# A hybrid decoder step on one core: early splits for the last matrix product, and squares of the final norm by halves

## The chip, the cores and the metric

The kernel runs on one core of a Trainium2 chip. The metric is the device time of one execution in microseconds (us). A core has TensorE (PE, matrix products), VectorE (DVE), ScalarE (ACT), GpSimd (POOL) and SyncE (SP, which issues most DMAs); each works through its own queue in order, and they wait for one another by semaphores.

## The reference

One inference step of a one-layer decoder for 1024 new prompt tokens (behind 16 meta tokens) and 32 tokens of eight running sequences. Attention and a state-space mixer are added into the residual stream `h`; then come the squared-ReLU MLP and a last RMSNorm, which is where the change lies:

```python
def mix_and_mlp(h, ao, so, attn_out_g, w_out, norm2_g, w_up, w_down):
    mix = jnp.concatenate([rmsnorm(ao, attn_out_g), so], axis=-1)
    h = h + mix @ w_out
    u = jax.nn.relu(rmsnorm(h, norm2_g) @ w_up)
    return h + (u * u) @ w_down          # w_down: 4096 x 1024
...
y_prompt = rmsnorm(hp, norm_f_g)[:, N_META:]   # x / sqrt(mean(x*x) + 1e-6) * g, over 1024 features
y_sample = rmsnorm(hs, norm_f_g)
```

Everything is float32.

## The kernel before

Activations lie features by tokens: 128 features on the partitions, eight feature blocks `m` = 0 to 7, 1056 tokens on the free axis (`TM`), in halves of 528 (`TH`) and quarters of 264 (`TQ`, chosen by `two(c)`, c = 0 to 3; c = 0, 1 are the first half).

A float32 product is made from three products of rounded operands. An operand x is split into hi, a cast to the rounded type on ACT, and lo = x - hi, a subtraction on DVE; the products are hi·hi, hi·lo and lo·hi (`three`). So each weight block and each block of activations costs one cast and one subtraction before TensorE can use it.

The down projection `(u*u) @ w_down` is computed by a Strassen scheme with seven block products in the order `ORDER` = 1, 6, 7, 4, 5, 3, 2. Each has 16 steps k over the inner dimension. The up projection leaves its activations, already combined, in DRAM (`u7`). For products 1 to 3 in that order, `step_down` (L1390 and on) runs 8 accumulators of 264 tokens, all eight PSUM banks, and adds them to `h` on DVE after the last step (L1404). Product 4 completes features 4 to 7 of the first token half, product 5 features 4 to 7 of the second, product 3 features 0 to 3 of the second, and product 2, the last, features 0 to 3 of the first half.

Up to product 3 the loop over `down` fetches (`fetch_down`: a weight block of 256 KB into the ten-buffer ring `wdr`, a load of 264 KB of activations into the five-buffer ring `tr`) up to five steps ahead and splits (`prep_down`, L1210, L1211, L1547, L1548) up to two steps ahead. These DMAs are on SP's queue.

Product 2 is a loop of its own (`last`): three passes over the 16 steps, (c = 0, blocks 0 to 3), (c = 1, blocks 0 and 1), (c = 1, blocks 2 and 3). `prep_last` loads (`wdq`) and splits a weight block into `w2_k` (L1663 to L1666), kept for all three passes; `acts_last` loads (`trq`) and splits the activations, into `tsq` for c = 0 and into `kept2` (`tk`) for c = 1 (L1671 to L1674). These live in pool `w2p`, which takes the memory of the pools of the products before it, closed at the end of product 3.

The final norm works by token quarters. `final(c, tag)` squares eight feature blocks on ACT in two halves (L1557), adds them on DVE to one column block `ac` (L1560, L1562), sums over the partitions with three matmuls against ones (`b<-ones,ac` or `c<-ones,ac`), takes mean and power -1/2 (L310 on DVE, L311 on POOL), puts the result on the diagonals of three matrices (`dg`, L1576), spreads it over the partitions with three matmuls (`<-dg,ones`), multiplies block by block with gain and norm (L1586) and stores pairs of blocks to `y` (L1589). It is a generator: each `yield` hands control back to the loop, which resumes it once per step. Quarters 2 and 3 are begun in product 3 and go on in product 2; quarter 0 follows; quarter 1, complete only with the last matmul, has `final_last` (L1618 to L1657), which scales by the gain on ACT (L1625) and multiplies pairs of blocks by the norm (L1656).

The order that the code writes is not the order of the queues: the framework plans the order of each engine's instructions when the program is built, by the order written, by what each needs and by its own estimate of times. A matmul appears in the trace as L202 whatever it computes (helper `mm`), so the names of output and operands tell which it is. A float32 matmul (norm sums, spreads) leaves two records, a product matmul one.

Of the kernel before, what the change touches and what calls it, by code (L numbers as in the profile page):

```python
# [15 lines left out]
D = 1024  # L16
# [170 lines left out]
def f(ap):  # L187
    return ap.bitcast(F32)
# [3 lines left out]
def body(ctx: ExitStack, tc: tile.TileContext, xT, xm, win, wdt, wo, wu, wd, ck, cv, sc, st, sT, vec, consts,  # L192
# [8 lines left out]
    def mm(out, a, b, start, stop, on=False):  # L201
        PE.matmul(out, lhsT=a, rhs=b, start=start, stop=stop, skip_group_check=on)  # L202
# [35 lines left out]
    class Ahead:  # L238
# [68 lines left out]
    def rstd_of(out, ssq, n):  # L307

        w = out.shape[-1]
        DVE.tensor_scalar(out=out, in0=ssq, scalar1=1.0 / n, scalar2=EPS, op0=ALU.mult, op1=ALU.add)  # L310
        POOL.tensor_tensor(out=out, in0=out, in1=nhalf[:out.shape[0], :w], op=ALU.pow)  # L311
# [614 lines left out]
    def gained(m, out, x):  # L926

        ACT.activation(out=out, in_=x, func=AF.Copy, scale=vec[:, V_G2 + m:V_G2 + m + 1])
# [231 lines left out]
    def bank(tag):  # L1160
        return pp5.tile([128, 512], F32, name=tag, tag=tag, bufs=3 if tag == "b" else 2) if tag != "g" else gps()
# [386 lines left out]
        DVE.tensor_tensor(out=t[:, 1], in0=x, in1=f(t[:, 0]), op=ALU.subtract)  # L1548
        ready[i] = w, t

    def final(c, tag):

        hc = h[:, :, two(c)]
        q2 = hpool.tile([128, 8, TQ], F32, name="q2", tag="q2", bufs=2)
        acc = hpool.tile([128, TQ], F32, name=f"ac{c}")
        for n in (4, 0):
            ACT.activation(out=q2[:, n:n + 4], in_=hc[:, n:n + 4], func=AF.Square)  # L1557
            yield
            for w in (2, 1):
                DVE.tensor_tensor(out=q2[:, n:n + w], in0=q2[:, n:n + w], in1=q2[:, n + w:n + 2 * w], op=ALU.add)  # L1560
                yield
        DVE.tensor_tensor(out=acc, in0=q2[:, 0], in1=q2[:, 4], op=ALU.add)  # L1562
        for _ in range(3):
            yield
        pt = bank(tag)
        at = (0, 128, TQ - 128)
        for q, a in enumerate(at):
            mm(pt[:, q:q + 1], acc[:, a:a + 128], ones[:, 0:1], True, True)
        for _ in range(4):
            yield  # L1570
        rs = hpool.tile([128, 3], F32, name="rs3", tag="rs3", bufs=2)
        dg = hpool.tile([128, 3, 128], F32, name="dg3", tag="dg3", bufs=1)
        rstd_of(rs, pt[:, 0:3], D)
        for _ in range(2):
            yield
        DVE.tensor_tensor(out=dg, in0=ident.unsqueeze(1).broadcast_to([128, 3, 128]),  # L1576
                          in1=rs.unsqueeze(2).broadcast_to([128, 3, 128]), op=ALU.mult)
        for _ in range(4):
            yield
        ps = bank(tag)  # L1580
        for q, a in enumerate(at):
            mm(ps[:, a:a + 128], ones, dg[:, q, :], True, True)
        for _ in range(3):
            yield
        for m in range(8):
            DVE.scalar_tensor_tensor(out=hc[:, m], in0=hc[:, m], scalar=vec[:, V_GF + m:V_GF + m + 1], in1=ps[:, :TQ],  # L1586
                                     op0=ALU.mult, op1=ALU.mult)
            if m % 2:
                SP.dma_start(out=y[:, c, m - 1:m + 1], in_=hc[:, m - 1:m + 1])  # L1589
                yield  # L1590

    finals = [final(2, "b"), final(3, "b")]
    fetched = done = EARLY
    for i, (j, k) in enumerate(down):
        if i < EARLY:
            continue
        while done < min(i + 3, len(down)):
            while fetched < min(done + 3, len(down)):
                fetch_down(fetched)
                fetched += 1  # L1600
            prep_down(done)
            done += 1
        if k in (6, 8, 10, 12) and j in (1, 6, 7, 4):
            mh, th = INTO[j]
            m = 4 * mh + k // 2 - 3
            SP.dma_start(out=h[:, m, TH * th:TH * th + TH], in_=he[:, m, TH * th:TH * th + TH])
        if j == 3 and k in (2, 4, 6):
            for x in finals:
                next(x)
        step_down(i, *ready.pop(i))  # L1610


# [5 lines left out]
    def final_last():  # L1618

        hc = h[:, :, two(1)]  # L1620
        q2 = hpool.tile([128, 8, TQ], F32, name="q2", tag="q2", bufs=2)

        def gained(a, b):
            for n in range(a, b):
                ACT.activation(out=hc[:, n], in_=hc[:, n], func=AF.Copy, scale=vec[:, V_GF + n:V_GF + n + 1])  # L1625

        ACT.activation(out=q2[:, 4:8], in_=hc[:, 4:8], func=AF.Square)
        for n in (6, 5):
            DVE.tensor_tensor(out=q2[:, 4:n], in0=q2[:, 4:n], in1=q2[:, n:2 * n - 4], op=ALU.add)
        yield  # L1630
        gained(4, 8)
        yield
        ACT.activation(out=q2[:, 0:2], in_=hc[:, 0:2], func=AF.Square)
        DVE.tensor_tensor(out=q2[:, 0], in0=q2[:, 0], in1=q2[:, 1], op=ALU.add)
        DVE.tensor_tensor(out=q2[:, 4], in0=q2[:, 4], in1=q2[:, 0], op=ALU.add)
        yield
        gained(0, 2)
        yield
        at = (0, 128, TQ - 128)
        for n in (2, 3):  # L1640
            ACT.activation(out=q2[:, n], in_=hc[:, n], func=AF.Square)
        pt = bank("c")
        for q, a in enumerate(at):
            for n in (4, 2, 3):
                mm(pt[:, q:q + 1], q2[:, n, a:a + 128], ones[:, 0:1], n == 4, n == 3)
        rs = hpool.tile([128, 3], F32, name="rs3", tag="rs3", bufs=2)
        dg = hpool.tile([128, 3, 128], F32, name="dg3", tag="dg3", bufs=1)
        rstd_of(rs, pt[:, 0:3], D)
        gained(2, 4)
        DVE.tensor_tensor(out=dg, in0=ident.unsqueeze(1).broadcast_to([128, 3, 128]),  # L1650
                          in1=rs.unsqueeze(2).broadcast_to([128, 3, 128]), op=ALU.mult)
        ps = bank("c")
        for q, a in enumerate(at):
            mm(ps[:, a:a + 128], ones, dg[:, q, :], True, True)
        for m in (4, 6, 0, 2):
            DVE.tensor_tensor(out=hc[:, m:m + 2], in0=hc[:, m:m + 2], in1=ps[:, :TQ].unsqueeze(1).broadcast_to([128, 2, TQ]), op=ALU.mult)  # L1656
            (ACT if m in (6, 2) else SP).dma_start(out=y[:, 1, m:m + 2], in_=hc[:, m:m + 2])  # L1657

    w2 = []

    def prep_last(k):
        x = w2p.tile([128, 4, 128], F32, name="wdq", tag="wdq", bufs=4)
        SP.dma_start(out=x, in_=wd[k + 16, :, 0])  # L1663
        w = w2p.tile([128, 2, 4, 128], F32R, name=f"w2_{k}")
        ACT.copy(out=w[:, 0], in_=x)
        DVE.tensor_tensor(out=w[:, 1], in0=x, in1=f(w[:, 0]), op=ALU.subtract)  # L1666
        w2.append(w)

    def acts_last(c, k):
        x = w2p.tile([128, TQ], F32, name="trq", tag="trq", bufs=4)  # L1670
        SP.dma_start(out=x, in_=u7[k][:, SLOT[2], two(c)])  # L1671
        t = kept2[k] if c else w2p.tile([128, 2, TQ], F32R, name="tsq", tag="tsq", bufs=4)
        ACT.copy(out=t[:, 0], in_=x)
        DVE.tensor_tensor(out=t[:, 1], in0=x, in1=f(t[:, 0]), op=ALU.subtract)  # L1674
        return t

    last = [(c, k, ms) for c, ms in ((0, (0, 1, 2, 3)), (1, (0, 1)), (1, (2, 3))) for k in range(16)]
    tq = {}
    done = 0
    end = final_last()  # L1680
    for i, (c, k, ms) in enumerate(last):
        while done < min(i + 4, len(last)):
            if done < 16:
                prep_last(done)
            tq[done] = acts_last(last[done][0], last[done][1]) if done < 32 else kept2[last[done][1]]
            done += 1
        if k == 0:
            ps = {m: bank(t) for m, t in zip(ms, "ccgg" if c == 0 else "bb" if ms[0] == 0 else "bg")}
            if c == 1 and ms[0] == 0:
                finals.append(final(0, "c"))  # L1690
        t = tq.pop(i)
        for m in ms:
            for n, (a, b) in enumerate(three):
                mm(ps[m][:, :TQ], w2[k][:, a, m, :], t[:, b], k == 0 and n == 0, k == 15 and n == 2)
            if k == 15:
                hv_ = h[:, m, two(c)]
                DVE.tensor_tensor(out=hv_, in0=hv_, in1=ps[m][:, :TQ], op=ALU.add)
        if i in (20, 24, 36, 40):
            next(end)
        for x in finals[:1] if i < 4 else finals:  # L1700
            next(x, None)
    for x in finals:
        for _ in x:
            pass
# [19 lines left out]
```

## Time and profile before

| | |
|---|---|
| median of 3 runs | 1162.9 us (1159.93 to 1163.7) |
| profiled execution | 1160.95 us |
| its span, first to last instruction | 1159.2 us |
| mean granted TensorE clock | 0.985 |
| PE busy | 1121.8 us, 8393 instructions |
| DVE busy | 852.7 us, 1656 instructions |
| ACT busy | 555.9 us, 1169 instructions |
| POOL busy | 246.0 us, 258 instructions |
| DMA traffic | 177.64 MB, mean 153 GB/s |

A row of the timeline has start and duration in us, engine, line, operation, output <- inputs, partitions x elements, the number of merged instructions, and in brackets how long the engine stood idle before it and what ended that. `SPq` and `ACTq` are the queues that issue DMAs. A row of the groups has busy time and mean duration in ns, then the idle time before its instructions.

### The profile page before, as it was taken

Reading aid. Unit: us, or ns where it says so; the run is one execution under the profiler, and the core shown is the slowest. Engines: PE = TensorE matmul, PEld = TensorE weight load, DVE = VectorE, ACT = ScalarE, POOL = GpSimd, SP = SyncE. Lnnn points to the kernel's source line nnn. Section 1 sums busy time; section 2 is a strip of 40 time slices with the busy share of each in tenths; the row PEclk is TensorE's granted clock in tenths of the full one; section 3 lists DMA queues with packets and bytes.
Section 4 is the critical chain, followed back from the end, with each engine's and each line's share of the span. In section 5 each row is a group of like instructions: output and inputs, shape, how many; then the busy total and the mean of one; then the engine's idle time right before and its main releaser. Section 6 shows DMA issues by size and latency. Waiting matters only on the chain.

```text
span 1159.2 us, 21711 instructions
## 1 busy us (share of the span) xinstructions
PE 1121.8 (97%) x8393; PEld 1082.4 (93%) x8393; DVE 852.7 (74%) x1656; ACT 555.9 (48%) x1169; POOL 246.0 (21%) x258
## 2 busy tenths in 40 slices
PE   7999989999999999999999999999999999999896
PEld 7899979888888899999999999999999999999896
DVE  7666788997589966988777777766599656775584
ACT  7312465756476647854444434444444333343451
POOL 4533343534345556210000000000000000000200
PEclk8999999999999999999999999999999999999898
DMA  8311110101276567556553343424999653455273
GB/s 291 114 37 38 37 37 19 31 35 57 93 227 193 161 237 232 193 189 218 174 190 143 138 169 113 178 101 170 384 302 310 194 173 91 137 174 152 67 212 120
DMA packets 84424, 177.64 MB, mean 153 GB/s; under 512 B 10692, under 2 KB 32740, under 8 KB 82272
## 3 DMA queue, kind: packets, MB, share of 16 engines
q1 hardware_dynamic: 77264, 141.44, 39.2%
q0 software_dynamic: 6224, 33.74, 7.3%
q8 instruction: 66, 1.08, 0.4%
q10 hardware_dynamic: 832, 1.07, 0.3%
q14 instruction: 38, 0.31, 0.1%
HBM read 125.49 MB, written 50.72 MB: 152 GB/s over the span
## 4 chain that ended last, share of the span: by engine, by line
PE 65%; DVE 14%; DMA 6%; issue 5%; ACT 4%; POOL 2%; POOLq 0%; DVEq 0%; SPq 0%; ACTq 0%
PE g L202 36%; PE b L202 16%; PE c L202 9%; PE s L202 2%; DMA wraw<-in_wu 2%; PE o L202 1%; DVE bc L512 1%; DVE p L638 1%; DVE Qs L671 1%; POOL sq L924 1%; DMA wdr<-in_wd 1%; DVE xs L512 1%; ACT p L640 1%; PE y L202 1%; DMA wraw<-in_wo 1%
## 5 line engine op out<-in xcount | busy, mean ns | idle before, releaser
L202 PE MATMUL g<-acth,whi 128*128 128x384 f32 (+2 forms) x624 | 195.6, 335 | 1.4 <-ACT acth L396 1.4
L202 PE MATMUL g<-acth,wlo 128*128 128x384 f32 (+2 forms) x624 | 194.6, 333 | 1.5 <-ACT wlo L234 0.9
L202 PE MATMUL g<-actl,whi 128*128 128x384 f32 (+2 forms) x528 | 175.2, 332 | 1.0 <-DVE actl L397 0.9
L1547 ACT CAST ts<-tr 128x528 fp32r<-128x528 f32 x92 | 58.3, 633 | 137.9 <-PE b L202 119.1
L202 PEld LDWEIGHTS g<-acth,wlo 128*128 128x128 f32 x624 | 117.9, 193 | 4.4 <-issue 1.6
L202 PEld LDWEIGHTS g<-acth,whi 128*128 128x128 f32 x624 | 117.2, 191 | 4.0 <-issue 2.0
L1548 DVE TENSOR_TENSOR ts<-tr,ts 128x528 fp32r<-128x528 f32 x92 | 64.9, 705 | 62.8 <-ACT ts L1547 59.8
L202 PEld LDWEIGHTS g<-actl,whi 128*128 128x128 f32 x528 | 101.4, 192 | 3.0 <-DVE actl L397 1.9
L311 POOL TENSOR_TENSOR rs<-rs,nhalf 128x3 f32<-128x3 f32 x10 | 14.3, 1434 | 335.9 <-DVE rs L310 335.9
L1268 ACT COPY s<-g 128x264 f32<-128x264 f32 x90 | 33.9, 378 | 69.8 <-PE g L202 66.5
L1341 POOL DMA_DIRECT2D u<-u x16 | 8.5, 532 | 176.0 <-ACT u L1284 143.5
L225 POOL TENSOR_TENSOR wlo<-wraw,whi 128x1024 fp32r<-128x1024 f32 (+1 forms) x18 | 41.9, 2330 | 16.5 <-ACT whi L224 16.4
L1273 DVE TENSOR_TENSOR u<-b,s 128x264 f32<-128x264 f32 x64 | 27.1, 430 | 23.7 <-PE b L202 14.3
L1278 ACT ACTIVATE u<-u 128x528 f32<-128x528 f32 x42 | 27.1, 646 | 29.5 <-DVE u L1277 29.5
L202 PE MATMUL b<-ts,w7y 128*128 128x264 f32 x279 | 39.3, 285 | 0.0
L202 PE MATMUL g<-ts,whi 128*128 128x264 f32 x279 | 38.9, 284 | 0.0
L202 PE MATMUL g<-ts,w7y 128*128 128x264 f32 x279 | 38.9, 283 | 0.0
L202 PE MATMUL b<-ts,whi 128*128 128x264 f32 x279 | 38.9, 284 | 0.0
L202 PE MATMUL g<-ts,wlo 128*128 128x264 f32 x270 | 38.0, 285 | 0.0
L202 PE MATMUL b<-ts,wlo 128*128 128x264 f32 x270 | 37.3, 282 | 0.0
L640 ACT ACTIVATE p<-p,nm 128x256 f32<-128x256 f32 (+1 forms) x64 | 31.3, 490 | 10.9 <-DVE nm L638 10.8
L202 PEld LDWEIGHTS b<-ts,w7y 128*128 128x128 f32 x279 | 36.1, 188 | 0.0
(549 smaller groups left out, 3362.0 us busy)
## 6 DMA issues: line engine op xcount, KB each, us to landing
tr<-u SPq DMA_DIRECT2D x92, 264.0 KB, 3.0
wraw<-in_wu SPq DMA_DIRECT2D x38, 512.0 KB, 4.3
u<-t POOLq DMA_DIRECT2D x16, 1056.0 KB, 5.7
wdr<-in_wd SPq DMA_DIRECT2D x64, 256.0 KB, 3.6
wraw<-in_win SPq DMA_DIRECT2D x16, 512.0 KB, 3.6
u<-u POOLq DMA_DIRECT2D x10, 792.0 KB, 3.6
wraw<-in_wo SPq DMA_DIRECT2D x24, 256.0 KB, 3.0
h<-he SPq DMA_DIRECT2D x16, 264.0 KB, 5.1
```

The costliest lines, as they stand in the source:

```text
L202: PE.matmul(out, lhsT=a, rhs=b, start=start, stop=stop, skip_group_check=on)
L225: eng.tensor_tensor(out=lo[:, k], in0=raw[:, k], in1=f(hi[:, k]), op=ALU.subtract)
L311: POOL.tensor_tensor(out=out, in0=out, in1=nhalf[:out.shape[0], :w], op=ALU.pow)
L512: DVE.scalar_tensor_tensor(out=acc, in0=cb[:, j:j + CL], scalar=cw_(j), in1=acc, op0=ALU.mult, op1=ALU.add)
L638: DVE.tensor_tensor_reduce(out=s_out, in0=ps, in1=mask, scale=-scale, scalar=nsink, op0=ALU.add, op1=ALU.min, accum_out=nm)
L640: ACT.activation(out=s_out, in_=s_out, func=AF.Exp, bias=nm, scale=-1.0, accum_out=sm)
L671: DVE.tensor_tensor(out=Q[oth, g, :, :rows], in0=src, in1=f(Q[own, g, :, :rows]), op=ALU.subtract)
L1268: ACT.copy(out=s[:, c], in_=ps[c][:, :TQ])
L1273: DVE.tensor_tensor(out=out[:, c], in0=ps[c][:, :TQ], in1=s[:, c], op=ALU.add)
L1278: ACT.activation(out=x, in_=x, func=AF.Square)
L1547: ACT.copy(out=t[:, 0], in_=x)
L1548: DVE.tensor_tensor(out=t[:, 1], in0=x, in1=f(t[:, 0]), op=ALU.subtract)
```

## The change

Four things change.

First, the operands of steps 0 to 3 of product 2's first pass (`NE` = 4) are loaded and split during product 3: weight blocks into ring `wdr`, 264 tokens of activations into ring `tr` (at steps 4 to 7), the splits (at steps 6 to 13) into tiles of a new pool `w2e` (`w2_0` to `w2_3`, `te0` to `te3`). `prep_last` and `acts_last` leave these steps out.

Second, the squares of features 4 to 7 are taken when these are complete: of quarters 0 and 1 during product 5, of quarters 2 and 3 during product 3 (`pre2`). The new generator `squared(c, n)` squares four blocks, adds them into `sums2[c]` and scales the blocks by the gain on ACT (`gained`); `final` squares the other four, and its last multiplication is by the norm alone, for two blocks at once (`normed`). Quarters 2, 3 and 0 start at steps 0, 6 and 16 of product 2.

Third, the diagonal matrices are three tiles with an instruction each (`diag`).

Fourth, the passes for c = 1 have blocks 0 to 2, then block 3. `final_last` sums blocks 0 to 2 during the last pass, keeps the scaled sum (`part`), and after the last matmul squares one block, sums it, and issues six matmuls of ones into an unused bank (`idle2`) ahead of the spread. The last stores hold 2, 2, 3 and 1 blocks.

```diff
-    def final(c, tag):
-        hc = h[:, :, two(c)]
...
+    sums2 = {}
+    def squared(c, n):
+        hc = h[:, n:n + 4, two(c)]
+        q2 = hpool.tile([128, 4, TQ], F32, name="q2", tag="q2", bufs=2)
+        ACT.activation(out=q2, in_=hc, func=AF.Square)
+        yield
+        DVE.tensor_tensor(out=q2[:, 0:2], in0=q2[:, 0:2], in1=q2[:, 2:4], op=ALU.add)
+        yield
+        if c in sums2:
+            DVE.tensor_tensor(out=q2[:, 0], in0=q2[:, 0], in1=q2[:, 1], op=ALU.add)
+            DVE.tensor_tensor(out=sums2[c], in0=sums2[c], in1=q2[:, 0], op=ALU.add)
+        else:
+            sums2[c] = hpool.tile([128, TQ], F32, name=f"ac{c}")
+            DVE.tensor_tensor(out=sums2[c], in0=q2[:, 0], in1=q2[:, 1], op=ALU.add)
+        yield
+        for m in range(4):
+            gained(c, n + m)
+            if m % 2:
+                yield
+    def gained(c, m):
+        hm = h[:, m, two(c)]
+        ACT.activation(out=hm, in_=hm, func=AF.Copy, scale=vec[:, V_GF + m:V_GF + m + 1])
+    def sum_tokens(tag, acc):
+        pt = bank(tag)
+        for q, a in enumerate(AT):
+            mm(pt[:, q:q + 1], acc[:, a:a + 128], ones[:, 0:1], True, True)
+        return pt
+    def diag(rs, q):
+        dg = hpool.tile([128, 128], F32, name="dg1", tag=f"dg{q}", bufs=2)
+        DVE.tensor_scalar(out=dg, in0=ident, scalar1=rs[:, q:q + 1], scalar2=None, op0=ALU.mult)
+        return dg
+    def spread(tag, dgs):
+        ps = bank(tag)
+        for a, dg in zip(AT, dgs):
+            mm(ps[:, a:a + 128], ones, dg, True, True)
+        return ps
+    def normed(c, ps, m, n):
+        hm = h[:, m:m + n, two(c)]
+        DVE.tensor_tensor(out=hm, in0=hm, in1=ps[:, :TQ].unsqueeze(1).broadcast_to([128, n, TQ]), op=ALU.mult)
+    def final(c, tag, waits):
+        yield from squared(c, 0)
+        pt = sum_tokens(tag, sums2[c])
+        # waits[0] yields, rstd_of, waits[1] yields, three diag, waits[2] yields, spread, waits[3] yields
...
+        for m in range(0, 8, 2):
+            normed(c, ps, m, 2)
+            SP.dma_start(out=y[:, c, m:m + 2], in_=h[:, m:m + 2, two(c)])
+            yield
+    w2e = ctx.enter_context(pool("w2e"))
+    NE = 4
...
+    pre2 = {5: [x for c in (0, 1) for x in [squared(c, 4)]], 3: [x for c in (2, 3) for x in [squared(c, 4)]]}
     for i, (j, k) in enumerate(down):
...
-        if j == 3 and k in (2, 4, 6):
-            for x in finals:
-                next(x)
+        if j in pre2 and k > 2:
+            next(pre2[j][k // 9], None)
+        if j == 3 and 4 <= k < 4 + NE:
+            raw2[k - 4] = block(k - 4, 0, 1)
+            rawt[k - 4] = dn.tile([128, TH], F32, name="tr", tag="tr", bufs=5)
+            SP.dma_start(out=rawt[k - 4][:, 0:TQ], in_=u7[k - 4][:, SLOT[2], two(0)])
+        if j == 3 and 6 <= k < 6 + 2 * NE:
+            n, x = (k - 6) // 2, (k - 6) % 2
+            if x:
+                tq[n] = w2e.tile([128, 2, TQ], F32R, name=f"te{n}")
+                split_acts(tq[n], rawt[n][:, 0:TQ])
+            else:
+                split_last(w2e, n, raw2[n])
         step_down(i, *ready.pop(i))
...
     def final_last():
+        ACT.activation(out=q2[:, 0:3], in_=hc[:, 0:3], func=AF.Square)
+        for n in (0, 1, 2):
+            DVE.tensor_tensor(out=sums2[1], in0=sums2[1], in1=q2[:, n], op=ALU.add)
...
+        pt = sum_tokens("c", sums2[1])
...
+        DVE.tensor_scalar(out=part, in0=pt[:, 0:3], scalar1=1.0 / D, scalar2=EPS, op0=ALU.mult, op1=ALU.add)
+        yield
+        ACT.activation(out=q2[:, 3], in_=hc[:, 3], func=AF.Square)
+        pt = sum_tokens("c", q2[:, 3])
+        for _ in range(6):
+            mm(idle2[:, 0:128], ones, ones, True, True)
...
+        DVE.scalar_tensor_tensor(out=rs, in0=pt[:, 0:3], scalar=1.0 / D, in1=part, op0=ALU.mult, op1=ALU.add)
+        POOL.tensor_tensor(out=rs, in0=rs, in1=nhalf[:, 0:3], op=ALU.pow)
+        gained(1, 3)
+        ps = spread("c", [diag(rs, q) for q in range(3)])
+        for m, n, q in ((4, 2, SP), (6, 2, ACT), (0, 3, SP), (3, 1, ACT)):
+            normed(1, ps, m, n)
+            q.dma_start(out=y[:, 1, m:m + n], in_=hc[:, m:m + n])
...
-    last = [(c, k, ms) for c, ms in ((0, (0, 1, 2, 3)), (1, (0, 1)), (1, (2, 3))) for k in range(16)]
+    last = [(c, k, ms) for c, ms in ((0, (0, 1, 2, 3)), (1, (0, 1, 2)), (1, (3,))) for k in range(16)]
...
+    finals = [final(2, "b", (3, 2, 3, 2)), final(3, "b", (3, 2, 3, 2)), final(0, "c", (3, 2, 2, 2))]
...
-        if i in (20, 24, 36, 40):
+        if i == 33:
+            idle2 = bank("g")
+        if i in (33, 35, 37, 38, 41):
             next(end)
```

More of the change, by code (lines that the diff above doesn't have):

```diff
@@ L1549, in prep_down @@
         ready[i] = w, t
-    def final(c, tag):
-        hc = h[:, :, two(c)]
[L1554 to L1560, printed above, removed]
-                yield
-        DVE.tensor_tensor(out=acc, in0=q2[:, 0], in1=q2[:, 4], op=ALU.add)
-        for _ in range(3):
-            yield
+    sums2 = {}
@@ L1565, in final @@
+    def gained(c, m):
+        hm = h[:, m, two(c)]
+        ACT.activation(out=hm, in_=hm, func=AF.Copy, scale=vec[:, V_GF + m:V_GF + m + 1])
+    AT = (0, 128, TQ - 128)
+    def sum_tokens(tag, acc):
         pt = bank(tag)
-        at = (0, 128, TQ - 128)
-        for q, a in enumerate(at):
+        for q, a in enumerate(AT):
             mm(pt[:, q:q + 1], acc[:, a:a + 128], ones[:, 0:1], True, True)
-        for _ in range(4):
+        return pt
[3 more added lines that the diff above has]
+        return dg
@@ L1570, in final @@
+    def spread(tag, dgs):
[9 more added lines that the diff above has]
+        pt = sum_tokens(tag, sums2[c])
+        for _ in range(waits[0]):
             yield
         rs = hpool.tile([128, 3], F32, name="rs3", tag="rs3", bufs=2)
-        dg = hpool.tile([128, 3, 128], F32, name="dg3", tag="dg3", bufs=1)
@@ L1573, in final @@
         rstd_of(rs, pt[:, 0:3], D)
-        for _ in range(2):
+        for _ in range(waits[1]):
             yield
-        DVE.tensor_tensor(out=dg, in0=ident.unsqueeze(1).broadcast_to([128, 3, 128]),
-                          in1=rs.unsqueeze(2).broadcast_to([128, 3, 128]), op=ALU.mult)
-        for _ in range(4):
+        dgs = [diag(rs, q) for q in range(3)]
+        for _ in range(waits[2]):
             yield
-        ps = bank(tag)
-        for q, a in enumerate(at):
-            mm(ps[:, a:a + 128], ones, dg[:, q, :], True, True)
@@ L1583, in final @@
-        for _ in range(3):
+        ps = spread(tag, dgs)
+        for _ in range(waits[3]):
             yield
[L1585 to L1592, printed above, removed]
+        for m in range(0, 8, 2):
+            normed(c, ps, m, 2)
+            SP.dma_start(out=y[:, c, m:m + 2], in_=h[:, m:m + 2, two(c)])
+            yield
@@ new lines, in body, with split_last, split_acts @@
+    w2e = ctx.enter_context(pool("w2e"))
+    NE = 4
+    w2, raw2, rawt, tq = {}, {}, {}, {}
+    def split_last(p, k, x):
+        w2[k] = p.tile([128, 2, 4, 128], F32R, name=f"w2_{k}")
+        ACT.copy(out=w2[k][:, 0], in_=x)
+        DVE.tensor_tensor(out=w2[k][:, 1], in0=x, in1=f(w2[k][:, 0]), op=ALU.subtract)
+    def split_acts(t, x):
+        ACT.copy(out=t[:, 0], in_=x)
+        DVE.tensor_tensor(out=t[:, 1], in0=x, in1=f(t[:, 0]), op=ALU.subtract)
+    pre2 = {5: [x for c in (0, 1) for x in [squared(c, 4)]], 3: [x for c in (2, 3) for x in [squared(c, 4)]]}
@@ L1620, in final_last @@
         hc = h[:, :, two(1)]
[L1621 to L1629, printed above, removed]
+        q2 = hpool.tile([128, 4, TQ], F32, name="q2", tag="q2", bufs=2)
@@ L1630, in final_last @@
+        ACT.activation(out=q2[:, 0:3], in_=hc[:, 0:3], func=AF.Square)
+        for n in (0, 1, 2):
+            DVE.tensor_tensor(out=sums2[1], in0=sums2[1], in1=q2[:, n], op=ALU.add)
         yield
-        gained(4, 8)
+        for m in range(3):
+            gained(1, m)
         yield
-        ACT.activation(out=q2[:, 0:2], in_=hc[:, 0:2], func=AF.Square)
-        DVE.tensor_tensor(out=q2[:, 0], in0=q2[:, 0], in1=q2[:, 1], op=ALU.add)
-        DVE.tensor_tensor(out=q2[:, 4], in0=q2[:, 4], in1=q2[:, 0], op=ALU.add)
+        pt = sum_tokens("c", sums2[1])
@@ L1636, in final_last @@
         yield
-        gained(0, 2)
         yield
[L1639 to L1645, printed above, removed]
-        rs = hpool.tile([128, 3], F32, name="rs3", tag="rs3", bufs=2)
-        dg = hpool.tile([128, 3, 128], F32, name="dg3", tag="dg3", bufs=1)
@@ L1648, in final_last @@
[L1648 to L1657, printed above, removed]
@@ L1659, in body @@
-    w2 = []
+        part = hpool.tile([128, 3], F32, name="rp3")
+        DVE.tensor_scalar(out=part, in0=pt[:, 0:3], scalar1=1.0 / D, scalar2=EPS, op0=ALU.mult, op1=ALU.add)
[4 more added lines that the diff above has]
+            mm(idle2[:, 0:128], ones, ones, True, True)
+        rs = hpool.tile([128, 3], F32, name="rs3", tag="rs3", bufs=2)
+        DVE.scalar_tensor_tensor(out=rs, in0=pt[:, 0:3], scalar=1.0 / D, in1=part, op0=ALU.mult, op1=ALU.add)
@@ L1663, in prep_last @@
         SP.dma_start(out=x, in_=wd[k + 16, :, 0])
[L1664 to L1667, printed above, removed]
+        split_last(w2p, k, x)
     def acts_last(c, k):
@@ L1672, in acts_last @@
         t = kept2[k] if c else w2p.tile([128, 2, TQ], F32R, name="tsq", tag="tsq", bufs=4)
-        ACT.copy(out=t[:, 0], in_=x)
-        DVE.tensor_tensor(out=t[:, 1], in0=x, in1=f(t[:, 0]), op=ALU.subtract)
-        return t
-    last = [(c, k, ms) for c, ms in ((0, (0, 1, 2, 3)), (1, (0, 1)), (1, (2, 3))) for k in range(16)]
-    tq = {}
+        split_acts(t, x)
+        return t
+    last = [(c, k, ms) for c, ms in ((0, (0, 1, 2, 3)), (1, (0, 1, 2)), (1, (3,))) for k in range(16)]
     done = 0
     end = final_last()
+    finals = [final(2, "b", (3, 2, 3, 2)), final(3, "b", (3, 2, 3, 2)), final(0, "c", (3, 2, 2, 2))]
     for i, (c, k, ms) in enumerate(last):
         while done < min(i + 4, len(last)):
-            if done < 16:
+            if NE <= done < 16:
                 prep_last(done)
-            tq[done] = acts_last(last[done][0], last[done][1]) if done < 32 else kept2[last[done][1]]
+            if done >= NE:
+                tq[done] = acts_last(last[done][0], last[done][1]) if done < 32 else kept2[last[done][1]]
             done += 1
         if k == 0:
-            ps = {m: bank(t) for m, t in zip(ms, "ccgg" if c == 0 else "bb" if ms[0] == 0 else "bg")}
-            if c == 1 and ms[0] == 0:
-                finals.append(final(0, "c"))
+            ps = {m: bank(t) for m, t in zip(ms, "ccgg" if c == 0 else "bbg" if ms[0] == 0 else "b")}
         t = tq.pop(i)
@@ L1697, in body @@
                 DVE.tensor_tensor(out=hv_, in0=hv_, in1=ps[m][:, :TQ], op=ALU.add)
-        if i in (20, 24, 36, 40):
+        if i == 33:
+            idle2 = bank("g")
+        if i in (33, 35, 37, 38, 41):
             next(end)
-        for x in finals[:1] if i < 4 else finals:
-            next(x, None)
+        for x, at in zip(finals, (0, 6, 16)):
+            if i >= at:
+                next(x, None)
     for x in finals:
```

## The prediction

> **What bounds the kernel now.** I read the page first, then busy time by stretch, then the waits, then the order of instructions around the stretch that stood out. From the page:
>
> ```profile
> span 1159.2 us, 21711 instructions
> PE 1121.8 (97%) x8393; PEld 1082.4 (93%) x8393; DVE 852.7 (74%) x1656; ACT 555.9 (48%) x1169; POOL 246.0 (21%) x258
> PEclk8999999999999999999999999999999999999898
> ```
>
> TensorE is the bound: 97% of the span. What it could still give lies where it is idle or slow, and the clock row shows two such places late: slice 38 (it reads 8) and the end. The change touches only the last three products, so I cut that part into stretches (busy time of PE, its weight loads, DVE, ACT and POOL with their instructions, the granted clock, the DMA share, GB/s):
>
> ```profile
> 993.00:1040.40 47.40, 47.40 (x392) 47.40 (x391) 34.08 (x58) 18.77 (x33) 0.00 (x0) 1.00 0.57 171
> ...
> 1040.40:1087.30 46.90, 46.90 (x386) 46.72 (x384) 24.22 (x44) 17.23 (x28) 0.00 (x0) 1.00 0.35 103
> 1087.30:1089.40 2.10, 0.04 (x1) 0.00 (x0) 2.03 (x6) 1.25 (x2) 0.00 (x0) 1.00 0.00 0
> 1089.40:1094.40 5.00, 2.72 (x12) 2.63 (x13) 3.31 (x8) 3.98 (x7) 0.99 (x1) 0.50 0.00 0
> 1094.40:1099.70 5.30, 5.30 (x25) 5.30 (x26) 5.30 (x13) 3.88 (x9) 4.60 (x1) 0.51 0.83 256
> 1099.70:1110.80 11.10, 11.10 (x93) 11.10 (x93) 8.57 (x17) 7.99 (x18) 1.05 (x1) 1.00 0.91 276
> ...
> 1146.40:1159.20 12.80, 3.85 (x25) 3.35 (x23) 3.75 (x8) 1.59 (x4) 0.85 (x1) 0.67 0.25 85
> ```
>
> Product 5 (to 1040.4) and product 3 (to 1087.3) fill TensorE without a gap. Between product 3 and product 2 there are 7.1 us with 12 tiny matmuls, then 5.3 us of product 2 at a granted clock of 0.51. From 1099.7 on TensorE is full again, and the last 12.8 us are a tail. The order on the queues there:
>
> ```profile
> 1065.75 0.43 SPq L1663 DMA_DIRECT2D wdq<-in_wd  x1
> ...
> 1086.81 0.53 PE L202 MATMUL b<-ts,whi 128*128 128x264 f32 x3
> 1089.41 1.44 PE L202 MATMUL b<-ones,ac 128*128 128x1 f32 x6 [2.08 <-DVE ac L1562]
> ...
> 1093.12 1.44 PE L202 MATMUL b<-ones,ac 128*128 128x1 f32 x6 [2.27 <-DVE ac L1562]
> 1094.42 0.79 PE L202 MATMUL c<-tsq,w 128*128 128x264 f32 x2
> ...
> 1086.38 1.09 ACT L1557 ACTIVATE q<-h 128x1056 f32<-128x1056 f32 x1 [7.14 <-DVE h L1404]
> 1087.84 1.08 ACT L1557 ACTIVATE q<-h 128x1056 f32<-128x1056 f32 x1 [0.37 <-DVE h L1404]
> 1089.45 1.09 ACT L1557 ACTIVATE q<-h 128x1056 f32<-128x1056 f32 x1 [0.53 <-DVE ac L1562]
> 1090.44 0.60 ACT L1665 CAST w<-wdq 128x512 fp32r<-128x512 f32 x1
> ```
>
> The weights of product 2's first step were requested at 1065.75, yet their cast runs at 1090.44: it stands on ACT's queue behind three squares of the final norm, the first of which waits 7.14 us for product 3's results. TensorE in turn takes the two norm sums, which wait for DVE (2.08 and 2.27 us), ahead of product 2. So the gap comes from the order of the queues, not from a lack of data.
>
> **The change part by part.** *Four steps split early.* Casts and subtractions of steps 0 to 3 move into product 3, into buffers of their own, so product 2 can start where product 3 ends, 1087.34 (1086.81 + 0.53). Prices at full clock:
>
> ```profile
> 1101.39 0.73 PE c L202 x6
> ...
> 1120.94 0.83 PE L202 MATMUL b<-dg,ones 128*128 128x128 f32 x6
> 1121.53 6.58 PE L202 MATMUL b<-tk,w 128*128 128x264 f32 x52
> ...
> 1128.86 0.72 PE L202 MATMUL c<-ones,ac 128*128 128x1 f32 x6
> ```
>
> A product matmul costs 0.73/6 = 0.122 us; a group of three norm matmuls (six records), spread or sum, holds TensorE 0.59 us from its start to the next product matmul. Before, 1087.34 to 1099.70 is 12.36 us for 24 product matmuls (the rest of the 25 records is an edge) and two sums. After: 24 x 0.122 + 2 x 0.59 = 4.11. Gain 8.25 us. The order of the pieces does not matter to this as long as PE does not wait.
>
> What that moves, on each queue. Into product 3: on SP eight DMAs (four of 256 KB, four of 132 KB), on ACT four casts of 0.61 and four of 0.41, on DVE four subtractions of 0.69 and four of 0.43; into products 5 and 3 also eight scalings of 0.51 each, and into product 5 the squares of features 4 to 7 of two token groups (1.09 each) with two adds (0.70 for 528 columns, as the subtraction L1548, and 0.43 for 264):
>
> ```profile
> L1666 DVE TENSOR_TENSOR w<-wdq,w 128x512 fp32r<-128x512 f32 x15 | 10.3, 689 | 1.2 <-ACT w L1665 0.5
> L1674 DVE TENSOR_TENSOR tsq<-trq,tsq 128x264 fp32r<-128x264 f32 x16 | 6.9, 430 | 2.3 <-ACT tsq L1673 2.3
> L1665 ACT CAST w<-wdq 128x512 fp32r<-128x512 f32 x14 | 8.6, 613 | 0.4 <-DMA wdq<-in_wd 0.4
> L1673 ACT CAST tsq<-trq 128x264 fp32r<-128x264 f32 x14 | 5.8, 412 | 5.7 <-PE g L202 5.4
> L1625 ACT ACTIVATE h<-h,vec 128x264 f32<-128x264 f32 x4 | 2.0, 512 | 0.0
> ...
> 1044.96 20.74 SPq L1521 DMA_DIRECT2D tr<-u  x8
> ...
> tr<-u SPq DMA_DIRECT2D x2, 264.0 KB, 2.7
> L1548 DVE TENSOR_TENSOR ts<-tr,ts 128x528 fp32r<-128x528 f32 x92 | 64.9, 705 | 62.8 <-ACT ts L1547 59.8
> ```
>
> Product 3 on ACT: 17.23 + 4 x 1.02 + 8 x 0.51 = 25.4 of 46.9 us; on DVE 24.22 + 4 x 1.12 = 28.7 of 46.9. Product 5: ACT 18.77 + 2 x 1.09 + 8 x 0.51 = 25.0, DVE 34.08 + 2 x 1.13 = 36.3, of 47.4. All hidden, TensorE being full there. DMA share 0.35 has room too. The shared resource is the ring of five `tr` buffers, of which the early activations hold up to four, and on SP's queue their loads stand between the step loads. The eight issues of the row start some 20.4/7 = 2.9 us apart, one per step, and the last ends at 1065.70, over six steps ahead of its use in the last 2.9 us of product 3; the split wants its data two steps ahead. If the four stay held, the step loads after them go one at a time, each in about 4.4 us (issue 0.4, as the row at 1065.75, landing 2.7, a cast of 0.6 like L1665's, subtraction 0.71): 1.5 us more than a step. Three of them, 13 to 15, come after the last early load, and the lead of four steps (11.7 us) covers their 4.5. I take 0; ends 0 and 2.0 us (a lead used up before the last of them, and an issue on top).
>
> *Step 4 onward* is still split in product 2. Its cover is the four steps already made: 48 x 0.122 = 5.86 us, with the sums 7.0, so it is due between 1093.2 and 1094.4. On ACT the second square ends at 1088.92; if all eight scalings of the two finished groups go first (4.1), the casts end at 1094.0 and the subtraction at 1094.7. At 1094.42 the trace starts a step with the products that need the casts alone. So even the worst order of the scalings is 0.3 us late at most, for the later products of one step; I take 0, nearest to that. Ends: 0 (scalings behind the casts) and 2.0 us (four scalings' time more).
>
> *Squares by halves, scaling on ACT.* In product 2 DVE gets four multiplications of 0.63 per group (2.54 in the rows below) for eight; the three-column matrix (0.56) becomes three of 128x128, which the trace does not show: between 0.16 (128x3) and 0.43 (128x264), by size 0.16 + (0.56 - 0.16)/3 = 0.29 each. DVE was busy 8.57 of 11.1 us there, hidden; 0.
>
> *Last pass of one block.* The 384 matmuls stay 384. One sum more stands inside the passes: +0.59. DVE waits for it with the new scaled partial sum, and behind that on DVE stands only the last block's add, some 4 us later. The tail, from these rows:
>
> ```profile
> 1145.90 0.52 PE L202 MATMUL g<-tk,w 128*128 128x264 f32 x3
> 1146.46 0.43 DVE L1697 TENSOR_TENSOR h<-h,g 128x264 f32<-128x264 f32 x1
> 1146.57 0.78 ACT L1641 ACTIVATE q<-h 128x264 f32<-128x264 f32 x2 [8.56 <-DVE h L1697]
> 1147.04 2.08 PE L202 MATMUL c<-ones,q 128*128 128x1 f32 x16 [0.50 <-ACT q L1641]
> 1149.16 0.16 DVE L310 TENSOR_SCALAR rs<-c 128x3 f32<-128x3 f32 x1 [2.27 <-PE c L202]
> 1149.47 0.85 POOL L311 TENSOR_TENSOR rs<-rs,nhalf 128x3 f32<-128x3 f32 x1 [14.37 <-DVE rs L310]
> 1150.35 0.56 DVE L1650 TENSOR_TENSOR dg<-cs,rs 128x384 f32<-128x384 f32 x1 [1.03 <-POOL rs L311]
> 1151.05 1.62 PE L202 MATMUL c<-dg,ones 128*128 128x128 f32 x6 [1.93 <-DVE dg L1650]
> 1152.71 2.54 DVE L1656 TENSOR_TENSOR h<-h,c 128x528 f32<-128x528 f32 x4 [1.81 <-PE c L202]
> ```
>
> Let E be the end of the last product matmul (1146.42). Before, the spread ends at E + 6.25. After: add to E + 0.47, one square to 0.90, three sum matmuls (0.72) from 0.98 to 1.70, DVE to 1.90, POOL 2.05 to 2.90, three matrices of 0.29 from 2.93 to 3.80, the last spread matmul (0.28, a third of the full-clock 0.83) to 4.19. Gain 2.06. The six filler matmuls are twelve records, 1.2 us at full clock, done at 2.9 before the first matrix at 3.22; at half clock (1.62/6 each) they and the spread take 4.9 us from 1.70 and the gain becomes a loss of 0.3. TensorE works until 1.70 here, so I take full clock. The four multiplications and stores: same bytes; 0.
>
> *Sum*: -8.25 + 0.59 - 2.06 = -9.7 us. On the profiled execution (1160.95 us, span 1159.2) that is 1151.2; that execution lies 1.95 us below the median 1162.9, so on the median 1153.2.
>
> **The rivals.** *Step 4 comes late.* Two us of waiting, and by the rows of the stretches the clock falls: after 2.1 us without product matmuls it was 0.50 from 1089.4 and stayed there for 10.3 us, through the sums and 24 product matmuls. Those took 5.28 us (1094.42 to 1099.70) instead of 2.93, so 2.35 more. Gain 9.7 - 4.4 = 5.3: 1157.6. For it: the eight scalings on ACT; against it: 5.86 us of cover. Chance 0.12.
>
> The Trainium skill, "TensorE: Matmul & The Clock Gate", section "Why this matters for your kernels", asks that no gap between bursts be longer than about 3 us, which puts a wait of 2 us on the safe side. By that rule this rival would cost its 2.0 us alone and end at 1155.2, inside the forecast's own range, and its 0.12 would go to the forecast. The row at 1087.30 disagrees: 2.1 us sufficed.
>
> *The sums block.* Norm matmuls hold up all that stands behind them on PE until DVE delivers, as at 1089.41 and 1093.12. If the planned order has product 2's two sums ahead of DVE by as much again, the wait and the half clock return (8.25 of the gain): 1161.5. Or the new partial sum does it: after the third block DVE owes three adds (0.43 each), three square adds (0.43 each) and four multiplications of the other group (2.54), 5.1 us, in a pass of 48 x 0.122 = 5.86; placed five steps (1.8 us) into it, it waits 3.3, and the other 33 matmuls at half clock cost 4.0: 1160.5. Against it: the sum at 1128.86 and the spread at 1120.94 passed without a wait. Chance 0.08.
>
> *The splits do not come early.* If ACT's queue has them behind the squares again, only the third square (1.09) leaves the gap, beside the tail's 2.06 less 0.59: gain 2.6, 1160.3. For it: the cast at 1090.44; against it: ACT idle for 29.7 of product 3's 46.9 us. Chance 0.04.
>
> *Product 3 starves (slower).* If the early activations are asked for so soon, and held so long, that the step loads lose their whole lead, they run at the ring's pace of 4.4 us: from step 7 to 15 nine steps of 1.5 more are 13.5 us, 1166.7. It decides from 9.7/1.5, some seven such steps, on. For it: four of five buffers; against it: the lead above. Chance 0.05.
>
> **How the numbers follow.** The forecast has 0.71; its own range is 1150 (the three matrices at 0.16, and the runs' offset of 1.95 smaller) to 1156.5 (one of the 2 us ends, and some of the runs' spread). A difference of 0.3%, 3.5 us, is about what a measurement can tell here: the three runs lie between 1159.93 and 1163.7. Faster by more (under 1159.4): 0.71 and the late step 4's 0.12, less 0.01 for its far end: 0.82. Within: 0.08 + 0.04 + 0.01 = 0.13. Slower: 0.05. The range 1150 to 1159.3 takes in the late step 4 and leaves out the last three rivals.
>
> **What would show it.** Right: product 2's first matmul (on `te`, not `tsq`) within 0.3 us of product 3's last; clock 1.00 through to the tail; casts of `te` between 1052 and 1085; one 0.39 us square in the tail and a spread within 4.5 us of the last product matmul. Wrong: PE idle behind `ac`, or ACT casts of step 4 later than 1094, or the clock at 0.50 anywhere in product 2; or PE gaps in product 3 behind `tr`.

## The result and the profile after

The changed kernel takes 1151.8 us (median of 4 runs, 1150.55 to 1152.0) against 1162.52 before (1159.93 to 1163.7; the three runs of the table ahead and a fourth): ratio 0.9908, 95% interval 0.9887 to 0.9929. The profiled execution took 1152.0 us with a span of 1150.2.

The same rows of the page, after:

```profile
span 1150.2 us, 21730 instructions
PE 1115.8 (97%) x8399; PEld 1076.4 (94%) x8399; DVE 850.5 (74%) x1654; ACT 566.5 (49%) x1192; POOL 239.5 (21%) x258
PEclk9899999999999999999999999999999999999998
```

The dip of the clock in slice 38 is gone, the one in the last slice is not. Busy time by stretch (PE, weight loads, DVE, ACT, POOL, then clock, DMA share, GB/s): products 5 and 3, product 2's pass for c = 0, its passes for c = 1, the tail:

```profile
992.70:1040.10 47.40, 47.40 (x392) 47.40 (x390) 36.05 (x61) 25.50 (x45) 0.00 (x0) 1.00 0.62 185
1040.10:1087.00 46.90, 46.90 (x387) 46.90 (x386) 27.96 (x52) 22.43 (x41) 0.00 (x0) 1.00 0.43 123
1087.00:1110.40 23.40, 23.40 (x197) 23.40 (x196) 19.39 (x46) 17.99 (x41) 2.23 (x2) 1.00 0.58 178
1110.40:1138.50 28.10, 28.10 (x235) 28.03 (x234) 17.45 (x41) 8.91 (x19) 0.91 (x1) 1.00 0.51 160
1138.50:1150.20 11.70, 3.72 (x25) 3.21 (x23) 3.82 (x9) 0.94 (x2) 0.85 (x1) 0.65 0.28 93
```

TensorE is full from product 5 to the last product matmul at a clock of 1.00, though ACT and DVE have more to do in products 5 and 3. The order at the boundary, and the tail:

```profile
1085.79 1.26 PE L202 MATMUL b<-ts,whi 128*128 128x264 f32 x9
1086.08 1.09 ACT L1557 ACTIVATE q<-h 128x1056 f32<-128x1056 f32 x1 [7.14 <-DVE h L1404]
1086.88 0.89 PE L202 MATMUL c<-te,w 128*128 128x264 f32 x6
...
1088.85 1.07 ACT L1557 ACTIVATE q<-h 128x1056 f32<-128x1056 f32 x1
1089.82 0.60 ACT L1629 CAST w<-wdq 128x512 fp32r<-128x512 f32 x1
...
1092.67 0.90 PE L202 MATMUL c<-tsq,w 128*128 128x264 f32 x6
...
1095.59 0.72 PE L202 MATMUL b<-ones,ac 128*128 128x1 f32 x6
...
1135.47 3.05 PE L202 MATMUL b<-tk,w 128*128 128x264 f32 x23
1138.36 1.28 PE L202 MATMUL g<-ones 128*128 128x128 f32 x10
1139.02 0.42 ACT L1690 ACTIVATE q<-h 128x264 f32<-128x264 f32 x1 [4.40 <-DVE h L1735]
1139.50 0.83 PE L202 MATMUL c<-ones,q 128*128 128x1 f32 x6
1140.19 0.47 PE L202 MATMUL g<-ones 128*128 128x128 f32 x2
1141.55 0.68 DVE L1588 TENSOR_SCALAR dg<-cs,rs 128x128 f32<-128x128 f32 x3 [1.03 <-POOL rs L1697]
1141.98 1.56 PE L202 MATMUL c<-dg,ones 128*128 128x128 f32 x6 [1.33 <-DVE dg L1588]
```

ACT still waits 7.14 us for product 3's results with casts behind it, as before. What changed is that TensorE does not need those casts: it takes step 0 (`te`) while product 3 drains, reaches the first late step at 1092.67 without a wait, and takes the norm sums when their input is ready. In the tail ten of the twelve filler records run ahead of the last sum, so TensorE is idle for 1.33 us before the spread, which runs at half speed (1.56 us).

Two measures serve from here on. The *body* goes from the end of product 3 to the end of the last product matmul, the *tail* from there to the span's end. Before: body 59.08 (1087.34 to 1146.42), tail 12.78. After: 51.47 (1087.05 to 1138.52) and 11.68. So of the 9.0 us by which the span is shorter, 7.61 lie in the body, 1.10 in the tail, 0.29 ahead of both. TensorE is as full as before up to the end of product 3, and that end moves between 1085.2 and 1090.7 us from profile to profile of all the kernels here; that is most of the scatter of the times, and body and tail are free of it. The tail has a smaller scatter of its own: from the end of the last multiplication to the end of the span, where the last stores run, it takes 3.7 to 4.1 us (3.95 before, 4.07 after, 3.70 in `early3` below with the tail of the kernel before).

### The profile page after: what moved, and what is told of

The parts are those of the page before. It is cut to its first block, busy times and chain, and to the rows that moved or that the text cites. A ratio compares the mean times of both kernels' runs of the same rounds, so it can differ in the third digit from the quotient of the medians.

```text
span 1150.2 us, 21730 instructions
## 1 busy us (share of the span) xinstructions
PE 1115.8 (97%) x8399; PEld 1076.4 (94%) x8399; DVE 850.5 (74%) x1654; ACT 566.5 (49%) x1192; POOL 239.5 (21%) x258
## 4 chain that ended last, share of the span: by engine, by line
PE 71%; DVE 14%; issue 5%; DMA 5%; ACT 4%; POOL 1%; POOLq 0%; SPq 0%; DVEq 0%; ACTq 0%
PE g L202 40%; PE b L202 17%; PE c L202 9%; PE s L202 2%; PE o L202 1%; DVE bc L512 1%; DVE p L638 1%; DVE xs L512 1%; ACT p L640 1%; DVE Qs L671 1%; DMA cb<-in_xT 1%; DMA wdr<-in_wd 1%; DVE Sd L1534 1%; DVE cb L437 1%; PE y L202 1%
## 5 line engine op out<-in xcount | busy, mean ns | idle before, releaser
L311 POOL TENSOR_TENSOR rs<-rs,nhalf 128x3 f32<-128x3 f32 x9 | 9.0, 996 | 312.8 <-DVE rs L310 312.7
```

## The experiments

Two theories. A: the early splits carry the gain, since TensorE no longer waits for queues. B: lighter queues carry it, since the squares of features 4 to 7 are out of product 2.

**No early step** (`ne0`).

```diff
-    NE = 4
+    NE = 0
```

> The changed kernel with no step split early (NE = 0), all else as changed. Theory A, the early splits carry the gain: product 2 again waits for its first casts, which the changed kernel's ACT queue reaches about 2.8 us after product 3's end; I expect a gap of 3 to 4 us, the granted clock at 0.50 for some 5 us after it (2.3 us more), so +5.5 to +6.5 us on the changed kernel: 1157.3 to 1158.3 us. Theory B, the lighter queues carry it (squares of features 4 to 7 out of product 2): at most +2 us, 1153.8.

Measured 1161.44 us, ratio to before 0.9998 (0.9981 to 1.0015). Timeline of PE, and the stretches with the clock:

```profile
core 0 of [0], span 1161.2 us
1089.45 1.25 PE L202 MATMUL b<-ts,whi 128*128 128x264 f32 x9
1092.77 0.83 PE L202 MATMUL b<-ones,ac 128*128 128x1 f32 x6 [2.07 <-DVE ac L1563]
1094.44 0.51 PE L202 MATMUL c<-tsq,w 128*128 128x264 f32 x2 [0.84 <-ACT tsq L1633]
...
1096.89 1.25 PE L202 MATMUL c<-tsq,w 128*128 128x264 f32 x4 [1.71 <-DVE tsq L1634]
...
1146.70 3.04 PE L202 MATMUL b<-tk,w 128*128 128x264 f32 x23
...
1153.21 1.62 PE L202 MATMUL c<-dg,ones 128*128 128x128 f32 x6 [1.33 <-DVE dg L1588]
```

```profile
1090.70:1092.80 2.10, 0.03 (x1) 0.03 (x1) 1.95 (x5) 2.07 (x6) 0.00 (x0) 1.00 0.00 0
1092.80:1096.90 4.10, 1.55 (x11) 1.26 (x11) 2.27 (x7) 4.10 (x10) 0.88 (x1) 0.78 0.00 0
1096.90:1101.50 4.60, 4.60 (x21) 4.60 (x22) 4.60 (x11) 3.00 (x7) 0.00 (x0) 0.50 0.73 203
```

Body 59.04, tail 11.46: the body is that of the kernel before to 0.04 us, with the lighter queues in place (and with the new partial sum, 0.59 us, in it, so they are worth 0.6 us there at most). Theory B falls. The loss in the body is 7.57 us, above the 5.5 to 6.5 expected: the waits add up to 4.62 us (2.07, 0.84 and 1.71), since I had left out the last, in which the later products of the first step wait for DVE's subtraction.

**Early splits alone** (`early3`): the kernel before, with the change's `w2e`, `split_last`, `split_acts` and the loads and splits in product 3, for three steps (four need 4 x (4096 + 2112) bytes, 24.25 KB per partition, beside square buffers twice as large as the change's).

```diff
+    w2e = ctx.enter_context(pool("w2e"))
+    NE = 3
...
+        if j == 3 and 4 <= k < 4 + NE:
+            raw2[k - 4] = block(k - 4, 0, 1)
...
+                split_last(w2e, n, raw2[n])
```

> The kernel before with steps 0 to 2 split early and nothing else changed (three, because a fourth does not fit beside the old, larger square buffers). Theory A: product 2 starts within 0.3 us of product 3's end and the two norm sums come later in the queue; its cover is 36 matmuls, 4.4 us, while the fourth step's cast stands behind three squares on ACT as before, so a wait of 0 to 2 us there: 1154.5 to 1157.5 us, 5 to 8 below the kernel before. Theory B: the old squares still crowd ACT and DVE, less than 2.5 us below it, over 1160.

Measured 1154.76 us, ratio 0.9941 (0.992 to 0.9962). Timeline:

```profile
core 0 of [0], span 1152.4 us
1087.86 1.26 PE L202 MATMUL b<-ts,whi 128*128 128x264 f32 x9
1088.95 0.90 PE L202 MATMUL c<-te,w 128*128 128x264 f32 x6
...
1093.79 1.40 PE L202 MATMUL b<-ones,ac 128*128 128x1 f32 x12
...
1139.35 0.52 PE L202 MATMUL g<-tk,w 128*128 128x264 f32 x3
```

Body 50.75, tail 12.53. The early splits alone give the whole gain of the body, and 0.72 us beyond, of which 0.59 is the new partial sum, which is not in it. From product 3's end to its last product matmul it gains 8.33 us on the kernel before, where the prediction had 8.25; the wait of 0 to 2 us at the fourth step did not come. Body and tail together are 63.28 us; the changed kernel has 63.15 (and 62.48 in two further profiles below). So the other parts add 0.1 to 0.8 us here, by profiles in which the last stores alone differ by 0.3; what else they do is make room for the fourth step. The interval of the runs overlaps those of the changed kernel (0.9887 to 0.9929 above, 0.9881 to 0.9944 and 0.9898 to 0.9937 below), so the runs do not tell the two apart.

**Two steps, one step** (`ne2`, `ne1`): `NE = 2` and `NE = 1`.

> The changed kernel with two steps split early (NE = 2). Cover 24 matmuls, 2.9 us, and one norm sum; casts of step 2 at about 2.8 us after product 3's end. Theory A: a wait of 0.5 to 1.5 us. If a wait that short leaves the clock at 1.00, +0.5 to +1.5 us (1152.3 to 1153.3); if the clock falls as it did after 2.1 us before, 2 to 2.5 us more (1154.5 to 1155.8). Theory B: no change, 1151.8.

> The changed kernel with one step split early (NE = 1). From product 3's end to the last product matmul the changed kernel took 51.47 us, two early steps 52.32, none 59.04. Cover here 12 matmuls, 1.46 us; by the changed kernel's trace the norm sum's input is ready 2.0 us after product 3's end and the next step's casts end at 3.7, so pieces of waiting of 0.5, 1.0 and 0.7 us. If waits of that size leave the clock at 1.00 (each TensorE gap short, work between them): 53.5 to 54.2 us. If the clock falls as with none: 55.5 to 57.5 us.

Two: 1152.46 us, ratio 0.9935 (0.991 to 0.9959), body 52.32, tail 11.01. One: 1157.41 us, 0.9964 (0.9947 to 0.9981), body 58.09, tail 10.73. Timeline of two, then of one with its stretches:

```profile
core 0 of [0], span 1149.6 us
1085.01 1.26 PE L202 MATMUL b<-ts,whi 128*128 128x264 f32 x9
1090.01 0.51 PE L202 MATMUL c<-tsq,w 128*128 128x264 f32 x2 [0.29 <-ACT tsq L1633]
...
1135.54 3.05 PE L202 MATMUL b<-tk,w 128*128 128x264 f32 x23
```

```profile
core 0 of [0], span 1155.7 us
1085.62 1.26 PE L202 MATMUL b<-ts,whi 128*128 128x264 f32 x9
...
1088.96 0.83 PE L202 MATMUL b<-ones,ac 128*128 128x1 f32 x6 [0.64 <-DVE ac L1563]
1090.62 0.51 PE L202 MATMUL c<-tsq,w 128*128 128x264 f32 x2 [0.83 <-ACT tsq L1633]
...
1093.08 1.25 PE L202 MATMUL c<-tsq,w 128*128 128x264 f32 x4 [1.71 <-DVE tsq L1634]
...
1141.92 3.05 PE L202 MATMUL b<-tk,w 128*128 128x264 f32 x23
```

```profile
1091.40:1093.10 1.70, 0.02 (x1) 0.02 (x1) 1.70 (x5) 1.70 (x6) 0.00 (x0) 0.77 0.00 0
1093.10:1099.00 5.90, 5.90 (x27) 5.90 (x28) 5.26 (x12) 3.58 (x8) 0.00 (x0) 0.50 0.75 213
```

The gain is not proportional to the early steps: body 59.04, 58.09, 52.32, 51.47 us for 0, 1, 2 and 4. With two, TensorE waits 0.29 us, the body is 0.85 us longer than with four, and the clock stays; the runs agree with theory A's lower case. With one, three waits add up to 3.18 us, none over 1.71, and the clock falls to 0.50. I had expected 57.5 at most and three waits of 2.2 together; the last one was 1.71 instead of 0.7, again DVE's subtraction.

**The last pass of one block taken back** (`pairs`): passes over blocks 0 and 1, then 2 and 3, for c = 1; the partial sum over two.

```diff
-(1, (0, 1, 2)), (1, (3,))
+(1, (0, 1)), (1, (2, 3))
...
-        ACT.activation(out=q2[:, 3], in_=hc[:, 3], func=AF.Square)
-        pt = sum_tokens("c", q2[:, 3])
+        for n in (2, 3):
+            ACT.activation(out=q2[:, n], in_=hc[:, n], func=AF.Square)
+        pt = bank("c")
+        for q, a in enumerate(AT):
+            for n in (2, 3):
+                mm(pt[:, q:q + 1], q2[:, n, a:a + 128], ones[:, 0:1], n == 2, n == 3)
```

> The changed kernel with the passes of the kernel before for c = 1 (blocks 0 and 1, then 2 and 3) and the partial sum over two blocks. Theory: the last pass of one block buys one square (0.36 us) and three sum matmuls (0.59 us) in the tail and nothing in the body: body 51.3 to 51.6 us, tail 12.6 us with the clock fallen at the spread, 11.9 without, against 11.68 of the changed kernel with it fallen. Rival: the tail is set by the chain from the norm to the stores and does not notice: 11.7.

Measured 1152.67 us, ratio 0.992 (0.9888 to 0.9951); body 51.96 (1087.32 to 1139.28), tail 11.92, the spread 1.01 us. The tail answers to the theory with the clock up (it was granted 0.83 during the spread). The body is 0.5 us longer than that of one block, which neither foresaw. The trace of `pairs` has 0.45 us of it: at 1125.09 and 1126.66 TensorE's weight loads wait 0.28 and 0.17 us for the subtraction of `tk` (L1634), the first of whose casts had itself waited 2.23 us for its load `trq`; in the changed kernel no weight load waits there. With two blocks to a pass each step is shorter, so the activations of c = 1 are due sooner. Over both parts the last pass of one block is worth about 1.4 us against `after2` below, less than the runs can show.

**Fillers** (`nofill`, `fill_dep`, `fill2`, and the changed kernel again as `after2` and `after3`). `nofill` drops the six; `fill_dep` and `fill2` are one kernel, with fillers that read the last square:

```diff
-        for _ in range(6):
-            mm(idle2[:, 0:128], ones, ones, True, True)
+        for _ in range(8):
+            mm(idle2[:, 0:128], ones, q2[:, 3, 0:128], True, True)
```

> The changed kernel with eight filler matmuls that read the last square, so that they can only run behind it, instead of six that read ones and ran ahead of the last sum. Theory F, the clock falls because TensorE idles 1.3 us there: it stays at 1.00 until the spread, which takes 0.83 us instead of 1.56; the tail from the last product matmul to the span's end shortens by 0.6 to 0.7 us of 11.7, and the time is 1151.1 (not told from 1151.8 by the runs, but by the profile). Rival: the clock falls some 3.5 us after the last product matmul whatever the fillers do; spread 1.5 us or more, tail 11.7.

> The changed kernel without the six filler matmuls. Theory: five of the six ran ahead of the last sum, where TensorE's idle time is short anyway, so they do not hold the clock to the spread: spread 1.5 to 1.6 us, tail 11.6 to 11.9. Rival: what work there was kept the clock up for part of it, and without it the sum's three matmuls run slow as well (0.72 becomes 1.4): tail 12.4.

> The changed kernel once more, to see which of its stretches vary from run to run: body 51.4 to 51.6 us again; tail 11.0 us if the clock is still 1.00 when the spread starts, 11.7 if it has fallen, for the same idle time of 1.33 us before it; product 3's end anywhere within 3 us of 1087.

> The changed kernel with eight dependent fillers once more. So far the spread took 0.84 us with these in one profile, and with the change's own fillers 1.56, 0.91, 0.91, 0.91 and 1.62 us in five. Theory F (TensorE's idle time of 1.3 us sometimes loses the clock and sometimes not, work up to the spread never does): spread 0.84 us again, body 51.5, tail 11.0 us. Rival (one lucky look): 1.5 us and 11.7.

> The changed kernel a third time, on the same chip as the dependent fillers: body 51.5 us, tail 11.0 or 11.7 us by the clock at the spread; in the runs no difference from the dependent fillers that can be told (0 to 0.7 us of 1152).

Timelines of `fill_dep`, of `after2`, and of `nofill`:

```profile
core 0 of [0], span 1147.7 us
1133.65 3.04 PE L202 MATMUL b<-tk,w 128*128 128x264 f32 x23
1137.66 0.83 PE L202 MATMUL c<-ones,q 128*128 128x1 f32 x6 [0.97 <-ACT q L1690]
1138.35 2.03 PE L202 MATMUL g<-q,ones 128*128 128x128 f32 x16
1140.22 0.84 PE L202 MATMUL c<-dg,ones 128*128 128x128 f32 x6
```

```profile
core 0 of [0], span 1150.3 us
1136.24 3.05 PE L202 MATMUL b<-tk,w 128*128 128x264 f32 x23
...
1142.76 0.91 PE L202 MATMUL c<-dg,ones 128*128 128x128 f32 x6 [1.33 <-DVE dg L1588]
```

```profile
1143.43 1.62 PE L202 MATMUL c<-dg,ones 128*128 128x128 f32 x6 [1.66 <-DVE dg L1588]
```

| | spread, us | body | tail | ratio to before |
|---|---|---|---|---|
| changed kernel | 1.56 | 51.47 | 11.68 | 0.9908 (0.9887 to 0.9929) |
| after2 | 0.91 | 51.47 | 11.01 | 0.9913 (0.9881 to 0.9944) |
| after3 | 0.91 | 51.47 | 11.01 | 0.9917 (0.9898 to 0.9937) |
| nofill | 1.62 | 51.47 | 11.74 | 0.991 (0.9879 to 0.9941) |
| fill_dep | 0.84 | 51.46 | 11.01 | 0.9933 (0.991 to 0.9955) |
| fill2 | 0.84 | 51.47 | 11.06 | 0.9909 (0.9889 to 0.993) |

The body repeats to 0.01 us. After the same 1.33 us of idle time the clock has fallen by the spread in one of three profiles of the changed kernel. The kernels with fewer early steps have the same tail and the same 1.33 us: there it fell in `ne0` (1.62 us) and not in `ne1` and `ne2` (0.91 us); `pairs`, with 1.01 us, lies between. With work up to the spread it did not fall in two of two.

So theory F stands only as far as two profiles go, beside four of six that kept the clock without such work. The time since the last product matmul does not decide it: in the kernels of the table the spread starts 3.46 to 3.53 us after it, with the clock up and with the clock down. An idle time of 1.33 us does not decide it alone either. Whether the change's fillers help is not shown: `nofill` fell, with 1.66 us, but so did `ne0` with the fillers in it. The rival named for `nofill` is out: without fillers the last sum ran at full clock (0.83 us, as with them). Where the clock stays up, the dependent fillers gain nothing (tail 11.01 and 11.06 us against 11.01); where it falls, they would save up to 0.7 us, which the runs cannot tell: medians of 1153.48 (`fill_dep`) and 1152.45 us (`fill2`) against 1152.0 (`after2`) and 1153.44 (`after3`).

## Why the prediction was right, and where it was off

*The total.* Forecast -9.7 us. The profiled execution moved by 9.0 and the medians of the runs by 10.7; with product 3's end moving over 5.5 us, that the total came so near is in part luck. The stretches test the mechanism better.

*The boundary.* (The "12 tiny matmuls" between the products are 12 records of six matmuls; the sum is not touched by it.) The step "24 x 0.122 + 2 x 0.59 = 4.11, gain 8.25", less 0.59 for the partial sum, gave 7.66; the body shrank by 7.61. `ne0` and `early3` show that the early splits are the cause, from both sides.

*What was moved.* ACT in product 5: 25.0 foreseen, 25.50 measured; DVE 36.3 and 36.05. In product 3 DVE 28.7 and 27.96, ACT 25.4 and 22.43: three of the four early weight casts (0.62 us each) ran in product 5, before 1040; the rest of the difference is open. The `tr` ring did no harm: TensorE is full in both.

*Step 4.* "I take 0" held: 1092.67 without a wait. In the worst order I had let all eight scalings go ahead of the casts; four did, the others stood between the casts, and the first late cast ran at 1089.82.

*The tail* is the term that was mis-sized: 2.06 us foreseen, 1.10 in the profile and 1.77 in `after2` and `after3`. The chain up to the matrices was right to 0.1 us (last matrix at 3.71 after the last product matmul, foreseen 3.80). "TensorE works until 1.70 here, so I take full clock" failed: the fillers were planned ahead of the sum, TensorE idled, and the spread ended at 5.02 (profile) or 4.38 (`after2`) instead of 4.19. Even at full clock it is 0.19 late: the three spread matmuls took 0.91 us from 3.47 on, where I had only the last, 0.28 us, behind the last matrix. So the sign "a spread within 4.5 us" held in `after2` and `after3` and failed in the profile.

*The rivals.* None came in the changed kernel. The late step came when I provoked it: with one early step the body lost 6.6 us of its 7.6, more than the rival's 4.4, for waits of 3.2 us instead of 2. "The splits do not come early" was given a gain of 2.6 us; `ne0` has 1.4 in body and tail, and none that its runs can show. The square less on ACT was to shorten the body by 0.5 (1.09 less the partial sum's 0.59), and it shortened by 0.04; the tail gained 1.3 of 2.06.

*The clock rule.* The Trainium skill, "TensorE: Matmul & The Clock Gate", section "Why this matters for your kernels", bounds harmless gaps at about 3 us. The rows of `ne1` from 1091.40 on do not bear that out either: its longest wait is 1.71 us, and the clock was 0.50 behind it, though the three waits together last 3.18 us. Nor is the prediction's own reading, "2.1 us sufficed", a rule: behind 2.07 us in `ne0` the sum still ran at a clock of 1.00 (0.83 us, against 1.44 before).

## What to carry to other kernels

At the boundary of two products look first at which cast the queues put behind work that waits for the old product's end; a few steps prepared earlier, enough to cover that wait, were worth the whole gain of the body here, and more steps than that added little. Fillers that are to keep TensorE busy must depend on what they are to follow: without that the planner ran ten of twelve records ahead of it here. When totals scatter by several us, compare stretches between two fixed events of the trace: here the body repeats to 0.01 us in six profiles.

## What the hardware did that I had not expected

The clock can fall after waits shorter than 2 us. Three waits of 0.64, 0.83 and 1.71 us within 5 us sufficed in `ne1`, and one of 1.33 us in the tail lost it in two profiles of six. But a longer wait need not: behind 2.08 us the norm sum of the kernel before ran at 0.50, behind 2.07 us that of `ne0` ran at 1.00, and there the clock fell only in the stretch after it (0.78 in the mean from 1092.80 to 1096.90). So the length of one wait does not decide it. What does was not tried.
